# Layer boundary of a two-layer trunk: two tiles get the last expert block's rows from a product with a 0/1 matrix

## The chip, the cores and the metric

One core of one Trainium2 chip runs the whole kernel. The metric is the device time of one execution in microseconds. Before the change it is 2198.02 us, the median of three runs (2182.05 to 2208.55).

## What is computed

The reference is a decoder trunk of two layers on 1024 tokens of width 1024 in float32. Each layer is

```
h   = layer_norm(x) * (1 + sc1) + sh1
mix = concat(gating(h @ w_in), attention(h @ w_in), s5(h @ w_in)) @ w_out
x   = layer_norm(ALPHA * x + (1 + g1) * mix) * ln1_g + ln1_b
h2  = layer_norm(x) * (1 + sc2) + sh2
ffn = grouped_moe(h2)              # 16 experts, two for each token
x   = layer_norm(ALPHA * x + (1 + g2) * ffn) * ln2_g + ln2_b
```

The boundary between the layers is the last line of layer 0 with the first of layer 1: for each tile of 128 tokens one norm with `ln2_g`, `ln2_b`, and on its result another with layer 1's `sc1`, `sh1`. The product `h @ w_in` follows. The sum inside the last line is complete for a token only when both of its experts have added their rows.

## The kernel before

**Order of the work.** Every engine runs its instructions in the order in which the program emits them. That order comes from a planner (class `Flow`): tasks are generators with a priority (a lower number goes first), and the planner keeps its own clock of when each engine, transfer and buffer is free. A task that yields a time, an event or a buffer goes on when the planner's clock allows it. The planner's times decide the order alone; on the chip every instruction waits for its real inputs.

**End of layer 0.** Experts are taken in an order by their counts. Their tokens' rows of `h2` are gathered in blocks of 128 slots, go through gate, up (`expert`, L2033) and down (`down`, L2083), are weighted on VectorE, and are added to the running sum `xa` in DRAM by an indirect DMA of GpSimd (`add_rows`, L362). The last expert of the order, at place `HALVES`, has two blocks: the first holds tokens of the first half of the sequence (tiles 0 to 3), the second those of tiles 4 to 7. `settle` (L2591) notes the planner's time at which the adds of all other blocks are in (`settled[1]`), and then those of the first and of the second of these two blocks (`settled[0]`, `settled[2]`). It also sets `first_down`, when the first block's `down` task has ended; the splitting of layer 1's first weights is held until then (`hold`, L1033). Before layer 1 begins there is a loop with a run-time count for overfull experts (`over`, L2159), at which all engines meet.

**Entry of layer 1.** One task for each of the 8 tiles (`enter_on`, L1104, spawned at L2409 with priority 4.4): it waits for `settled[0]` (tiles 0 to 3) or `settled[2]` (tiles 4 to 7), loads 128 rows of `xa` (a slot of tag `hT`), takes mean and variance, applies `lg`, `lb` in two VectorE instructions, stores the result to `xres`, takes mean and variance again, and applies `sc`, `sh` in two VectorE instructions into a tile `t` of which there are two. Then eight PE transposes, each half copied and split into two parts by ScalarE and VectorE (`transpose_in`, L1054). Even tiles take their statistics on VectorE (`bn_stats`), odd ones on ScalarE (two passes with accumulation into a scratch half of the slot). The reciprocal root is seven small VectorE instructions (`rstd`, L393). With `steps` the task yields after each small instruction, so that several tiles' instructions interleave.

**The projection** (`project`, L1138, run by `first` at L2433) takes the tiles in order: for each, 24 products of 512 columns with the four units `uv` and 24 of 256 columns with the two units `us`. A unit is loaded into one of two buffers `raw` by SP's queue (`loader`) and split into two parts by ScalarE and VectorE (`splitter`, L1026).

**Buffers.** PSUM banks: three of kind A, two of B, two of Y, one of C. A block's `down` product takes both Y banks. The pool `hT` has 8 slots.

## Time and profile before

| | |
|---|---|
| Time, median of three runs | 2198.02 us (2182.05 to 2208.55) |
| The profiled execution's own time | 2191.28 us |
| Its span, first to last instruction | 2189.5 us |
| Mean granted TensorE clock | 0.942 of full speed |
| PE busy | 1931.7 us (88%) |
| DVE busy | 1191.8 us (54%) |
| ACT busy | 730.9 us (33%) |
| POOL busy | 317.8 us (15%) |

PE is TensorE's matmul side, PEld its weight loads, DVE VectorE, ACT ScalarE, POOL GpSimd, SP SyncE, whose queue issues most transfers. A busy share is an average over all stages. Almost every compute instruction goes through one of a few helpers, so its line is the helper's (L108 for DVE, ACT and POOL, L463 for products, L476 for transposes, L354 and L364 for transfers): one reads the groups by the names of their tiles. `bankA`, `bankB`, `bankC` and `bankY` are PSUM banks; `wu` and `hT` hold weights or activations; `xa` is the running sum in DRAM. The clock is given as a share of 2.4 GHz, so 0.50 is the lower level, 1.2 GHz. One fp32 product of 128x128 by 128x512 stands in the trace as two matmul records; a product of the split kind stands as one record.

### The profile page before, as it was taken

How to read it: one execution, taken by the hardware profiler on the slowest of the kernel's cores; microseconds unless marked ns; L12 is line 12 of the kernel's file. 1: busy time of each engine (PE TensorE's matmuls, PEld its weight loads, DVE VectorE, ACT ScalarE, POOL GpSimd, SP SyncE). 2: the span in 40 equal slices, each digit the busy share in tenths (PEclk: the TensorE clock that was granted, in tenths of full speed). 3: DMA queues.
4: the chain of work that ended last, by engine and by line, in shares of the span. 5: the costliest groups of instructions: out<-in, count | busy, mean ns of one | idle time of the engine just before them, and what ended most of it. 6: DMA issues, size and time to landing. Idle time of an engine off the chain costs nothing. (4 is left out here: it accounts for less than half of the span.)

```text
span 2189.5 us, 32472 instructions
## 1 busy us (share of the span) xinstructions
PE 1931.7 (88%) x12026; PEld 1343.3 (61%) x12026; DVE 1191.8 (54%) x2901; ACT 730.9 (33%) x1336; POOL 317.8 (15%) x304
## 2 busy tenths in 40 slices
PE   5988899999898999897867999999898999999882
PEld 3766676668663656556536877766685556665640
DVE  7757544556771754335368594445477432443636
ACT  2321144543321423324233424455223130332431
POOL 0014000100123323311001221020000111111010
PEclk9999999999999999999887999999899999999996
DMA  7566623245747799897763544331564678989782
GB/s 244 195 191 178 220 87 96 68 138 180 276 147 264 246 320 343 300 347 227 257 210 111 192 130 151 92 103 50 174 220 164 235 240 292 310 300 318 236 297 100
DMA packets 186822, 451.50 MB, mean 206 GB/s; under 512 B 28969, under 2 KB 80377, under 8 KB 169637
## 3 DMA queue, kind: packets, MB, share of 16 engines
q1 hardware_dynamic: 169584, 393.60, 51.3%
q0 software_dynamic: 15584, 55.24, 10.4%
q8 instruction: 96, 1.57, 0.3%
q10 hardware_dynamic: 1492, 0.56, 0.1%
q14 instruction: 66, 0.53, 0.1%
HBM read 366.66 MB, written 83.01 MB: 205 GB/s over the span
## 5 line engine op out<-in xcount | busy, mean ns | idle before, releaser
L463 PE MATMUL bankA<-wu,hT 128*128 128x512 f32 (+2 forms) x3250 | 832.3, 414 | 27.5 <-DMA hT<-mixT 12.8
L463 PEld LDWEIGHTS bankA<-wu,hT 128*128 128x128 f32 (+1 forms) x3250 | 565.9, 190 | 199.7 <-issue 67.7
L463 PE MATMUL bankA<-hT 128*128 128x512 f32 (+1 forms) x768 | 243.0, 482 | 3.0 <-DVE hT L108 1.9
L108 DVE TENSOR_TENSOR wu<-raw,wu 128x1024 fp32r<-128x1024 f32 x124 | 153.6, 1245 | 144.5 <-ACT wu L108 143.5
L108 ACT ACTIVATE hT<-bankB 128x512 fp32r<-128x512 f32 (+1 forms) x174 | 99.2, 594 | 354.5 <-PE bankB L476 335.0
L463 PE MATMUL bankY<-wu,hT 128*128 128x512 f32 (+1 forms) x500 | 187.7, 538 | 6.6 <-ACT hT L108 4.0
L108 ACT ACTIVATE wu<-raw 128x1024 fp32r<-128x1024 f32 x124 | 130.2, 1058 | 158.3 <-DMA raw<-in_exp_w_down_dram 33.4
L463 PEld LDWEIGHTS bankA<-hT 128*128 128x128 f32 (+1 forms) x768 | 131.5, 183 | 75.5 <-issue 48.6
L108 POOL TENSOR_TENSOR ada_w<-ada_w 128x512 f32<-128x512 f32 x84 | 118.4, 1409 | 351.9 <-ACT ada_w L108 342.8
L108 DVE TENSOR_TENSOR hT<-bankB,hT 128x512 fp32r<-128x512 f32 x114 | 75.8, 687 | 123.5 <-ACT hT L108 123.2
L463 PEld LDWEIGHTS bankY<-wu,hT 128*128 128x128 f32 (+1 forms) x500 | 93.4, 195 | 73.1 <-issue 52.0
L364 POOL DMA_INDIRECT xa<-g,rc_idx x40 | 70.7, 1767 | 459.5 <-DVE g L108 365.7
L463 PE MATMUL bankY<-hT 128*128 128x512 f32 (+1 forms) x404 | 117.5, 496 | 9.6 <-ACT hT L108 9.5
L108 DVE TENSOR_TENSOR hT<-raw,hT 128x1024 fp32r<-128x1024 f32 x57 | 70.4, 1238 | 87.9 <-ACT hT L108 87.3
L108 DVE SCALAR_TENSOR_TENSOR g<-bankY,rc_wsl,mod 128x512 f32<-128x512 f32 x68 | 48.4, 746 | 88.6 <-PE bankY L463 87.9
L463 PEld LDWEIGHTS bankY<-hT 128*128 128x128 f32 (+1 forms) x404 | 63.8, 179 | 48.4 <-issue 23.3
L108 ACT ACTIVATE ada_w<-ada_w,csel 128x512 f32<-128x512 f32 x96 | 67.5, 717 | 73.1 <-DMA ada_w<-in_ada_w_dram 71.4
L463 PE MATMUL bankC<-wu,hT 128*128 128x512 f32 (+1 forms) x260 | 83.4, 473 | 2.1 <-DVE wu L108 1.1
L108 ACT ACTIVATE hT<-raw 128x1024 fp32r<-128x1024 f32 x57 | 60.2, 1058 | 73.2 <-DMA raw<-in_exp_w_gate_dram 24.3
L108 ACT ACTIVATE hT<-hT,mx 128x256 f32<-128x256 f32 (+7 forms) x128 | 70.6, 557 | 6.3 <-DVE mx L108 6.2
L476 PE MATMUL bankB<-ident,hT 128*128 128x128 f32 x384 | 62.5, 289 | 7.1 <-ACT hT L108 3.9
L108 ACT ACTIVATE mhT<-bankB 128x512 f32<-128x512 f32 x32 | 19.1, 598 | 141.0 <-PE bankB L476 141.0
(495 smaller groups left out, 2608.7 us busy)
## 6 DMA issues: line engine op xcount, KB each, us to landing
ada_w<-in_ada_w_dram SPq DMA_DIRECT2D x160, 256.0 KB
raw<-in_exp_w_gate_dram SPq DMA_DIRECT2D x48, 512.0 KB
raw<-in_exp_w_up_dram SPq DMA_DIRECT2D x48, 512.0 KB
raw<-in_exp_w_down_dram SPq DMA_DIRECT2D x48, 512.0 KB
wu<-in_exp_w_up_dram SPq DMA_DIRECT2D x20, 1024.0 KB
wu<-in_exp_w_down_dram SPq DMA_DIRECT2D x19, 1024.0 KB
wu<-in_exp_w_gate_dram SPq DMA_DIRECT2D x19, 1024.0 KB
hT<-in_exp_w_up_dram SPq DMA_DIRECT2D x19, 1024.0 KB
```

Of the source, the lines that this page charges most:

```text
L108: f(*a, **k)
L364: self.nc.gpsimd.indirect_dma_start(out=rows, out_offset=bass.IndirectOffsetOnAxis(ap=ix, axis=0), in_=x, in_offset=None, compute_op=OP.add)
L463: self.nc.tensor.matmul(out, l, r, start=start, stop=stop, **kw)
L476: self.nc.tensor.transpose(out, x, self.ident[:k, :k] if perm is None else perm)
```

## The change

`enter_on` of tiles 0 and 1 (`HANDED` = 2) no longer waits for the first block of the last expert. It waits for `settled[1]`, reads its rows of `xa` without that block, and gets the block's share from PE: `place` builds for each of the two tiles a 128x128 matrix of zeros and ones (slot by token of the tile) in `rt["hx"]`; after the block's rows `y` are weighted, `down` multiplies each matrix with `y` into two Y banks, and `enter_on` adds the banks to its rows on VectorE and frees them. The scatter-add of that block is emitted only after both reads have been (`self.read`), and must not overwrite what they read. The two tasks get priority 0.5 in place of 4.4.

For all tiles: the slot of `x` is half as long; the tile `t` is taken before the first statistics instead of before the last affine step, and serves as ScalarE's scratch, so that every tile but tile 0 takes its statistics on ScalarE; tile i waits, ahead of its first affine step, until tile i-2's last affine step has been emitted (`entered`); tiles 0 and 1 run without `steps` and with fewer `pace` waits. In the planner every scatter-add of the kernel, in both layers, is taken to be done 6 us later.

```diff
--- before.py
+++ after.py
@@ -38,6 +38,8 @@
 EARLY = 2
 CAPS = (384,) + (256,) * 3 + (128,) * 2 + (64,) * 8 + (256,) + (128 * EARLY,)
 ALONE, HALVES, RANKED = 6, NE - 2, 5
+
+HANDED = 2
 BASE = [256 * EARLY + sum(CAPS[:p]) for p in range(NE - 1)] + [128 * EARLY]
 NPLAN = EARLY + sum(CAPS) // 128
 PAIRS = BASE[ALONE] // 128
@@ -363,7 +365,7 @@

         self.nc.gpsimd.indirect_dma_start(out=rows, out_offset=bass.IndirectOffsetOnAxis(ap=ix, axis=0), in_=x,
                                           in_offset=None, compute_op=OP.add)
-        return self.fl.dma("pool", rows, x, [ix])
+        return self.fl.dma("pool", rows, x, [ix]) + 6.0

     def to_row(self, dst, at, pool, tag):

@@ -443,6 +445,8 @@
             self.v.bn_aggr(mv[:, j], st.rearrange("p a b -> p (a b)"))
             if steps:
                 yield ("until", self.fl.busy["dve"])
+        if junk is not None and not steps:
+            yield self.fl.on(mv)
         rs = yield from self.rstd(tp, mv[:, :, 1], n, steps)
         return [(mv[:, j, 0:1], rs[:, j:j + 1]) for j in range(n)]

@@ -1103,29 +1107,45 @@

     def enter_on(self, l, i, tp, bc):

-        yield ("wait", self.settled[i * 2 // NT * 2])
-        x2 = yield ("tile", self.slots, [128, 2, D], F32, None)
-        x, junk = x2[:, 0], x2[:, 1] if i % 2 else None
+        yield ("wait", self.settled[1 if i < HANDED else i * 2 // NT * 2])
+        x = yield ("tile", self.slots, [128, D], F32, None)
         self.dma(x, self.xa[l - 1][i * 128:i * 128 + 128])
+        if i < HANDED:
+            self.unread -= 1
+            if not self.unread:
+                self.read.at = self.fl.now
+
+            pb, ev = self.handed[i]
+            yield ("wait", ev)
+            yield self.fl.on(x, *pb)
+            for n in range(2):
+                s = slice(n * 512, n * 512 + 512)
+                self.v.tensor_add(x[:, s], pb[n], x[:, s])
+            self.free(*pb)
         yield self.fl.on(x)
+        h = yield self.tile(tp, [128, D], F32, "t", 2)
         if i:
-            yield from self.pace(0.2)
-        st = yield from self.stats(tp, [x], D, junk, i > 0)
+            yield from self.pace(0.2, "act")
+        st = yield from self.stats(tp, [x], D, h if i else None, i >= 2)
         for k in ("lg", "lb"):
             yield ("wait", bc[k][1])
-        yield from self.pace(0.6)
+        if i > 1:
+            yield ("wait", self.entered[i - 2])
+        if i >= HANDED:
+            yield from self.pace(0.6)
         self.affine(x, x, st[0], bc["lg"][0], bc["lb"][0], x)
         yield self.fl.on(x)
         self.dma(self.xres[i * 128:i * 128 + 128], x)
         if i:
-            yield from self.pace(0.2)
-        st = yield from self.stats(tp, [x], D, junk, i > 0)
+            yield from self.pace(0.2, "act")
+        st = yield from self.stats(tp, [x], D, h if i else None, i >= 2)
         for k in ("sc", "sh"):
             yield ("wait", bc[k][1])
-        h = yield self.tile(tp, [128, D], F32, "t", 2)
-        yield from self.pace(0.6)
+        if i >= HANDED:
+            yield from self.pace(0.6)
         self.affine(h, x, st[0], bc["sc"][0], bc["sh"][0], h)
-        self.free(x2)
+        self.entered[i].at = self.fl.now
+        self.free(x)
         yield self.fl.on(h)
         yield from self.transpose_in(i, h)
         self.free(h)
@@ -1827,7 +1847,7 @@
         v.tensor_copy(r["ew"][:, a], tw[:, :, 1])
         self.ew_ready[j // 4].at = self.fl.on(r["ew"])[1]

-    def place(self, tp, xp):
+    def place(self, l, tp, xp):

         v, c, r = self.v, self.rc, self.rt
         mk = lambda s, sh, dt=F32: tp.tile(sh, dt, name="pl_" + s, tag="pl_" + s)
@@ -1912,6 +1932,13 @@
             self.free(oh, ob)
         at = mk("at", [128, NBLK])
         v.tensor_copy(at, pb[:, :NBLK])
+        if not l:
+
+            k, hx = BASE[HALVES] // 128, mk("hx", [128, HANDED])
+            r["hx"] = xp.tile([128, HANDED, 128], F32, name="hxs")
+            for i in range(HANDED):
+                v.tensor_scalar(hx[:, i:i + 1], at[:, k:k + 1], -1.0 - 128 * i, None, op0=OP.add)
+                v.tensor_scalar(r["hx"][:, i], c["i128"], hx[:, i:i + 1], None, op0=OP.is_equal)
         self.to_row(r["idx"], at, tp, "pl_t")
         self.idx_ready.at = self.fl.on(r["idx"])[1]
         v.tensor_scalar(at[:, PAIRS:NPLAN], at[:, PAIRS:NPLAN], c["hi"], None, op0=OP.mult)
@@ -2030,7 +2057,7 @@
                 self.mm(o[c], x[:, a, xk, c], u.part(b, uk), start and i == 0, stop and i == len(ps) - 1,
                         None if w == 128 else 0.43)

-    def expert(self, l, lanes, blocks, xes, ends, tp, early=False, keep=False, final=None):
+    def expert(self, l, lanes, blocks, xes, ends, tp, early=False, keep=False, final=None, hand=False):


         nu = len(lanes[0]) // 3
@@ -2074,13 +2101,13 @@
                                 self.free(gs[j])
                             if not early or xes[j].last:
                                 self.free(xes[j].tile)
-                            ends.append(self.fl.spawn(self.down(l, lanes, b, hid[j], pb[j], tp, work, final), 4))
+                            ends.append(self.fl.spawn(self.down(l, lanes, b, hid[j], pb[j], tp, work, final, hand), 4))
                     yield ("go",)
                 if not keep:
                     for u in us:
                         self.free(u.tile)

-    def down(self, l, lanes, b, hid, up, tp, work, final=None):
+    def down(self, l, lanes, b, hid, up, tp, work, final=None, hand=False):
         v, nu = self.v, len(lanes[0]) // 3
         yield self.fl.on(hid, up)
         v.tensor_mul(hid, hid, up)
@@ -2143,6 +2170,8 @@
         if early:
             for e in self.mix_done:
                 yield ("wait", e)
+        if hand:
+            yield ("wait", self.read)
         ix, xa = self.rt["eidx" if early else "idx"][:, b:b + 1], self.xa[l][:, :]
         if len(lanes) == 1:
             self.added.append(self.add_rows(xa, y, ix))
@@ -2150,6 +2179,13 @@

             self.add_rows(xa, y[0:64], ix[0:64])
             self.added.append(self.add_rows(xa, y, self.rt["idx2"][:, b - PAIRS:b - PAIRS + 1]))
+        if hand:
+            for i in range(HANDED):
+                pb, ev = self.handed[i]
+                pb += yield self.bank("Y", 2)
+                for n in range(2):
+                    self.mm(pb[n], self.rt["hx"][:, i], y[:, n * 512:n * 512 + 512], True, True)
+                ev.at = self.fl.now
         self.free(work)
         if b < EARLY:
             self.early_left -= 1
@@ -2392,7 +2428,7 @@
         self.hT_ready, self.s_ready, self.mix_done, self.chosen = ev(), ev(), ev(), ev(2)
         self.c_ready, self.b_left, self.left, self.late_left = Event(), [4] * NT, [4, 4], 2 * NT
         self.pa_open, self.kq_open, self.at_open, self.s5_go = ev(4)
-        self.vc, self.vc_ready = [None] * 2, ev(2)
+        self.vc, self.vc_ready, self.entered = [None] * 2, ev(2), ev()
         self.hT, self.q = [None] * NT, [None] * NT
         pa_s, kq_s = ExitStack(), ExitStack()
         b = SimpleNamespace(pa_s=pa_s, kq_s=kq_s, prep=None, sb=None)
@@ -2406,7 +2442,7 @@
             tp = self.pool(st, "prm", "right")
             loads = self.param_loads(tp)
         if l:
-            ins = [fl.spawn(self.enter_on(l, i, ln, bc), 4.4 + i / 100) for i in range(NT)]
+            ins = [fl.spawn(self.enter_on(l, i, ln, bc), (0.5 if i < HANDED else 4.4) + i / 100) for i in range(NT)]
         else:
             ins = [fl.spawn(self.enter(l, t, ln, bc), t[0]-2) for t in ((0,), (1,), (2, 3), (4, 5), (6, 7))]
         uv, us, ua = self.w_first
@@ -2568,7 +2604,7 @@
                 u.pools = self.wpools[:-1]
             self.g2 = self.mod(tp, l, 5, "g2")
             pl_s = ExitStack()
-            e = fl.spawn(self.place(self.pool(pl_s, "place", "right"), tp), 1)
+            e = fl.spawn(self.place(l, self.pool(pl_s, "place", "right"), tp), 1)
             fl.spawn(self.gather_first(l, 1, fx[EARLY:], [(tp, "g", 3)], tp), 0)
             runs = [early, fl.spawn(late_blocks(), 5.7)]
             for ps in ORDER:
@@ -2580,6 +2616,7 @@
             bh = [BASE[HALVES] // 128, BASE[HALVES] // 128 + 1]
             xh, written, first_up, first_down, emitted = ev(2), Event(), Event(), Event(), Event()
             settled = self.settled = ev(3)
+            self.read, self.unread, self.handed = Event(), HANDED, [([], Event()) for _ in range(HANDED)]
             for b, xe in zip(bh, xh):
                 fl.spawn(self.gather(l, b, xe, tp), 3)
             for u in ue[HALVES][4:]:
@@ -2606,7 +2643,7 @@
             def halves():
                 for k in range(2):
                     yield from self.expert(l, [ue[HALVES]], bh[k:k + 1], xh[k:k + 1], last, tp, keep=not k,
-                                           final=written if l else None)
+                                           final=written if l else None, hand=not l and not k)
                     if not k:
                         first_up.at = fl.now
             runs.append(fl.spawn(halves(), 5.5))
```

## Rows read from the trace of the kernel before

**Rows 1.** Waits, 1060 to 1250 us: who waited for whom; us, times, longest.
```profile
PE bankB L476 <- DVE t L108: 30.4, 2, 17.3
```

**Rows 2.** Timeline of PE, layer boundary: start, us, operation; idle before and releaser.
```profile
1106.43 7.03 PE L463 MATMUL bankA<-hT 128*128 128x512 f32 x16
...
1119.22 3.60 PE L463 MATMUL bankY<-wu,hT 128*128 128x512 f32 x8
...
1135.97 1.94 PE L476 MATMUL bankB<-ident,t 128*128 128x128 f32 x8 [13.15 <-DVE t L108]
...
1137.74 9.43 PE L463 MATMUL bankA<-wu,hT 128*128 128x512 f32 x48
...
1164.42 1.94 PE L476 MATMUL bankB<-ident,t 128*128 128x128 f32 x8 [17.26 <-DVE t L108]
...
1169.21 13.39 PE L463 MATMUL bankA<-wu,hT 128*128 128x512 f32 x60
...
1183.22 8.64 PE L463 MATMUL bankA<-wu,hT 128*128 128x512 f32 x48
...
1227.14 11.86 PE L463 MATMUL bankA<-wu,hT 128*128 128x512 f32 x61 [0.30 <-ACT hT L108]
```

**Rows 3.** Windows: length, busy us of PE, PEld, DVE, ACT, POOL; PE clock, DMA, GB/s.
```profile
1105.00:1240.00 135.00, 101.07 (x511) 80.03 (x510) 96.90 (x199) 54.38 (x104) 22.85 (x17) 0.86 0.48 154
...
1120.00:1180.00 60.00, 28.37 (x129) 22.98 (x128) 54.86 (x132) 19.86 (x42) 1.77 (x2) 0.69 0.51 178
...
1140.00:1150.00 10.00, 7.17 (x43) 6.20 (x41) 9.76 (x31) 6.81 (x16) 0.00 (x0) 0.99 0.46 181
...
1160.00:1170.00 10.00, 4.35 (x18) 3.88 (x19) 8.65 (x15) 2.20 (x4) 0.00 (x0) 0.50 0.14 56
```

**Rows 4.** Timeline of DVE, layer boundary.
```profile
1120.67 1.29 DVE L108 BATCH_NORM_STATS2 bn_s<-hT 128x6 f32<-128x512 f32 x2 [0.23 <-DMA hT<-xa]
...
1122.23 0.15 DVE L108 TENSOR_SCALAR rs_a<-bn_m 128x1 f32<-128x1 f32 x1
...
1126.21 1.40 DVE L108 SCALAR_TENSOR_TENSOR g<-bankY,rc_wsl,mod 128x512 f32<-128x512 f32 x2
...
1132.08 1.23 DVE L108 TENSOR_TENSOR wu<-raw,wu 128x1024 fp32r<-128x1024 f32 x1
...
1188.80 2.20 DVE L108 SCALAR_TENSOR_TENSOR t<-t,rs_y,mod 128x1024 f32<-128x1024 f32 x1
```

**Rows 5.** Timeline of POOL: a first gather, the last scatter-adds, a multiply-add of layer 1.
```profile
684.65 1.00 POOL L358 DMA_INDIRECT g<-h,rc_idx  x1 [0.15 <-issue]
...
1075.74 1.55 POOL L364 DMA_INDIRECT xa<-g,rc_idx  x1 [23.17 <-DVEq L2168]
...
1107.66 2.27 POOL L364 DMA_INDIRECT xa<-g,rc_idx  x1 [30.38 <-DVE g L108]
...
1190.28 1.87 POOL L108 TENSOR_TENSOR ada_w<-ada_w 128x512 f32<-128x512 f32 x1 [0.37 <-ACT ada_w L108]
```

**Rows 6.** Timeline of SP's DMA issues at the boundary.
```profile
1094.08 0.90 SPq L354 DMA_DIRECT2D mod<-modrow  x2
...
1108.55 1.52 SPq L354 DMA_DIRECT2D raw<-in_w_in_dram  x2
...
1117.45 1.76 SPq L354 DMA_DIRECT2D hT<-xa  x4
```

**Rows 7.** Groups of DVE, 1105 to 1240 us: operation, count, busy us, mean ns, idle before.
```profile
L108 DVE TENSOR_TENSOR wu<-raw,wu 128x1024 fp32r<-128x1024 f32 x9 | 11.2, 1259 | 11.3 <-ACT wu L108 11.3
```

**Rows 8.** Timeline of ACT: first and last instruction of an odd tile's statistics.
```profile
1129.28 1.04 ACT L108 ACTIVATE hT<-hT 128x1024 f32<-128x1024 f32 x1
...
1131.73 0.19 ACT L108 ACTIVATION_READ_ACCUMULATOR hT<-hT,bn_a 128x1 f32 x1
```

**Rows 9.** Timeline of DVE, layer 0's placing: the slot indices.
```profile
654.80 0.20 DVE L108 SCALAR_TENSOR_TENSOR rc_idx<-pl_at,pl_t 128x37 int32<-128x37 f32 x1
```

**Rows 10.** Timeline of DVE, last stage of layer 1.
```profile
2128.32 0.17 DVE L108 TENSOR_SCALAR rs_a<-bn_m 128x2 f32<-128x2 f32 x1 [9.01 <-ACT g L108]
```

## The prediction

> **What bounds the kernel now.** I read the page's shares first: PE is busy 88% of the span, DVE 54%. That says where the time goes on average, so the second view is the waits of the boundary, 1060 to 1250 us: PE stood 30.4 us in two pieces ahead of transposes that waited for DVE's tile `t` [rows 1]. The third is PE's timeline. The last block of layer 0 ends at 1122.8; tile 0's transposes start at 1135.97 after 13.15 us of idleness, its projection ends at 1147.17, then 17.26 us pass until tile 1's transposes at 1164.42; from 1169.21 PE is dense. Tile 7's projection is the first 48 of the 61 records from 1227.14, so it ends near 1227.14 + 48/61 x 11.86 = 1236.5 [rows 2]. The fourth is busy time by windows: from 1120 to 1180 DVE is busy 54.86 of 60 us, 91%, while PE is busy 28.37 [rows 3]. So the boundary is bound by DVE, which spends the first 60 us on norms of all tiles side by side while PE needs tile 1's. The reader should see two separate losses: tile 0 starts late, since its rows come back from DRAM only at 1120.67 [rows 4], 13 us after the block's scatter-add was issued at 1107.66 [rows 5]; and tile 1 is finished late, because tiles 2 to 7 share DVE with it.
>
> **The change, part by part.** I work out when tile 7's projection ends, against 1236.5.
>
> Start of DVE's work. The block's weighted rows are ready just before its add at 1107.66 [rows 5]. PE is then in the second block's up product, 16 records in 7.03 us from 1106.43 [rows 2]; the task gives PE away only after half of it, at 1109.9. Tile 0's product is two fp32 products, four records at 0.44 us: 1.8 us, so DVE can add at 1111.7. The two reads of `xa` need the last other add, issued at 1075.74 [rows 5], and stand on SP's queue behind the rows loaded at 1094.08; nothing follows there until 1108.55 [rows 6]. Before, four reads issued at 1117.45 [rows 6] let DVE start at 1120.67 [rows 4], 3.2 us later; even twice that puts the new ones in by 1102. They cost nothing; without that cover, the whole chain waits for them.
>
> DVE's work up to tile 7's transposed parts. In 1105 to 1240 DVE was busy 96.9 us [rows 3]. Tiles 2, 4 and 6 give six statistics to ACT: from 1120.67 to the first small instruction at 1122.23 is 1.56 us [rows 4], six are -9.4. Four adds out of PSUM come in; the nearest row is the weighting out of PSUM, two in 1.40 us at 1126.21 [rows 4], so +2.8. The first block's weighting lies ahead of the start: -1.4. Of nine splits of weights [rows 7] three lie behind the first projection, which needs six: at 1.23 us [rows 4], -3.7. The rest is 85.2 us.
>
> What share of the time DVE is busy. The bounds are 91% (the window with all tiles side by side) and 96.9/135 = 72% (the whole stage, where PE is the bound in its second half) [rows 3]. Two tiles `t` taken early mean two tiles in flight. From 1122.23 to 1126.21 a root and two affine steps take 3.98 us [rows 4], so a tile's DVE work is 2 x 3.98, with two part-subtractions from PSUM at 0.70 some 9.4 us. Its ACT statistics take 1129.28 to 1131.92, 2.64 us [rows 8], twice. A pair thus needs 18.8 us of DVE, and one tile's chain (9.4 + 5.3 + transposes 1.9 [rows 2]) is 16.6 us plus waits behind the other. I take 86%, nearer to 91%, because the work is the same: 85.2/0.86 = 99 us, to 1210.8. Tile 7 then needs its transposes, about 1.0 (half of the 1.94 at the lower clock), and 48 records at 8.64 [rows 2]: 1220. **Gain: 16 us.**
>
> Does PE allow that? Tile 0's chain took 1120.67 to 1135.97 [rows 2, 4]; from 1113.1 the same 15.3 us end at 1128.4. The weights' hold is released only after tile 1's product, about 1117 (another half product and 1.8 us) in place of 1107.7, so the sixth split, at 1132.08 before [rows 4], may be up to 10 us late; at worst tile 0's projection ends near 1144. Seven more tiles at 9.6 us end at 1211, before DVE's 1220. The hold therefore costs nothing unless DVE does better than 95%.
>
> Collisions with POOL. An affine step at 1188.80 took 2.20 us instead of 1.28 [rows 4]; POOL ran layer 1's multiply-adds, one from 1190.28 for 1.87 us [rows 5]. They are released by tile 3, which comes earlier, so more norms lie beside them; those met before are in the 96.9 already. I take 1 us, bounds 0 and 5 (0.92 us for about five more meetings). The Trainium skill ("SBUF — State Buffer", Who interferes with whom) says that a DVE instruction with two SBUF inputs and a POOL instruction that reads SBUF exclude each other for a whole instruction. The row agrees, and by that rule each meeting could cost up to 1.87 us, the sum losing 9 in place of 1.
>
> Costed at nothing. `place` gets four small DVE instructions, under 2 us, ahead of the slot indices; these are done at 655.0 [rows 9], and the first gather is issued at 684.65 [rows 5]. The products lengthen PE's queue by 3.5 us ahead of a 13.15 us gap. The second block's add, behind the first on POOL, is late by 4 to 7 us; it feeds tiles 4 to 7, needed after 1150. ACT takes 16 us more in a stage where it was busy 54.4 of 135 [rows 3]. The 6 us in the planner also reorder the last stage of layer 1, whose norms follow a scatter-add; no row shows that. There DVE waited 9.01 us behind ACT's statistics [rows 10]; later placing can add to that or fill it: -4 to +4, taken as 0.
>
> The sum is 15 us: 2191.3 - 15 = 2176.3 for the profiled execution. That lies 6.7 us under the median of 2198.0, so 2183 on the median's scale.
>
> **The rivals.** *DVE stays as dense as it was (chance 0.22).* At 91% the stage ends at 1111.7 + 93.6 + 9.6 = 1215; at best PE is the bound, with tile 0's projection over by 1140 and seven tiles at 9.6, 1207: a gain of 22 to 29 us, about 2173. For it: 91% was held for 60 us. Against: eight tiles in flight then, two now.
>
> *The reads come late, so the product gives no start (0.18).* The reads need free slots of `hT`. If there are none until the up weights' slots come free, when the 16 records end at 1113.5 [rows 2], the rows arrive near 1118, the block's add waits for them, and tiles 2 and 3 behind it: 6 us of start lost and a share near 80%, 85.2/0.8 = 106.5, end 1234: a gain of 2, so 2196.
>
> *Slower: two tiles in flight starve DVE (0.12).* DVE runs in order: an instruction waiting for ACT's statistics holds the other tile's ready ones, as for 9.01 us in the last stage [rows 10]. The break-even is 1236.5 = 1111.7 + 85.2/s + 9.6, a share s of 74%. PE would also idle ahead of each tile: the granted clock was 0.50 from 1160 to 1170, after the 17.26 us gap, against 0.99 from 1140 to 1150 [rows 3], and 60 records took 13.39 us, where 8.64 per 48 makes 10.8: 2.6 us for a restart [rows 2]. The last tile pays one. At 65%: 1111.7 + 131 + 9.6 + 2.6 = 1255, 18 us slower, 2216. The Trainium skill ("TensorE: Matmul & The Clock Gate", HAM oscillation) warns that matmuls fed in pieces with waits between fall back to the lower clock each time. The rows agree for single gaps; by it seven restarts at 2.6 us would cost PE 18 us, hidden as long as DVE is the bound.
>
> **How the numbers follow.** The forecast (share 80 to 91%, gain 8 to 22) has 0.48. Point: 2183. Range: from the dense rival at its best, 2169, with some of the runs' spread, 2163, to a share just past break-even, 2203. A measurement of this kernel can tell about 1%, 22 us. Faster by more, below 2176: most of the dense rival and the forecast's top with the runs' scatter, 0.32. Slower by more, past 2220, needs a share near 63%: 0.07. Within 1%: 0.61.
>
> **What would show it.** Right: DVE adds out of `bankY` near 1112; tile 0's transposes before 1131; tile 1's within 3 us of the end of tile 0's projection; DVE 80 to 91% busy from 1112 to 1205; dense PE from tile 1 on except gaps of 1 to 3 us that end on DVE `t`; tile 7's projection over near 1220. Wrong: reads of `xa` issued after 1105; a gap ahead of every tile with a clock below 1; DVE idle behind ACT; PE waiting for `wu`; a last stage of layer 1 longer or shorter by over 4 us.

## The result, and the profile after

The changed kernel takes **2174.67 us** (median of 4 runs, 2170.59 to 2178.52) beside 2202.56 us for the kernel before (4 runs): a ratio of 0.9897 [0.9861, 0.9933]. The forecast was 2183. The profiled execution took 2174.52 us (span 2172.7) against 2191.28, so 17 us went. Where they went is not where the forecast had them. I measure the **stage** from the end of the first block's weighting on DVE to ACT's reading of tile 7's last bank: 128.7 us before, 120.7 after. That is 8 us; the forecast had 16, less 1 for collisions. Another 14 us are gone before the boundary begins, and 5.5 us come back behind it.

POOL's timeline of the changed kernel shows the last other add and the two adds of the last expert:

```profile
1061.40 1.55 POOL L366 DMA_INDIRECT xa<-g,rc_idx  x1 [24.05 <-DVEq L2204]
1093.51 1.55 POOL L366 DMA_INDIRECT xa<-g,rc_idx  x1 [30.56 <-DVE g L110]
1122.31 1.55 POOL L366 DMA_INDIRECT xa<-g,rc_idx  x1 [27.25 <-DVE g L110]
```

Against [rows 5] the last other add is issued 14.3 us earlier and the block's 14.2 us earlier. Nothing of the boundary has happened when the first of them is issued. SP's timeline answers to [rows 6]:

```profile
1080.45 1.06 SPq L356 DMA_DIRECT2D hT<-xa  x2
...
1104.07 1.25 SPq L356 DMA_DIRECT2D hT<-xa  x2
```

The rows of tiles 0 and 1 are read ahead of the block's add. PE's timeline at the boundary answers to [rows 2]:

```profile
1095.54 1.88 PE L467 MATMUL bankY<-g,hxs 128*128 128x512 f32 x4
...
1100.69 1.88 PE L467 MATMUL bankY<-g,hxs 128*128 128x512 f32 x4
...
1106.60 1.13 PE L480 MATMUL bankB<-ident,hid 128*128 128x128 f32 x4 [4.03 <-DVE hid L110]
...
1116.03 1.04 PE L480 MATMUL bankB<-ident,t 128*128 128x128 f32 x8
...
1128.75 1.94 PE L480 MATMUL bankB<-ident,t 128*128 128x128 f32 x8 [2.49 <-DVE t L110]
...
1131.99 11.44 PE L467 MATMUL bankA<-wu,hT 128*128 128x256 f32 x59 [0.68 <-DVE wu L110]
1145.06 1.07 PE L480 MATMUL bankB<-ident,t 128*128 128x128 f32 x8 [1.62 <-DVE rs_a L110]
...
1191.24 1.94 PE L480 MATMUL bankB<-ident,t 128*128 128x128 f32 x8 [3.60 <-DVE rs_a L110]
1193.02 6.13 PE L467 MATMUL bankA<-wu,hT 128*128 128x512 f32 x18
...
1200.89 14.24 PE L467 MATMUL bankA<-wu,hT 128*128 128x512 f32 x84
```

The two gaps of [rows 2], 13.15 and 17.26 us, are gone. Gaps of 1.6 to 3.6 us ahead of single tiles stand in their place; `rs_a` as releaser is the small instruction that follows the tile's affine step on DVE. Tile 7's projection ends with the 78th of the last 84 records, near 1214.1, counted as in the forecast. The waits of the same stretch (1060 to 1250 us) answer to [rows 1]:

```profile
PE bankB L480 <- DVE rs_a L110: 8.0, 5, 3.6
PE bankB L480 <- DVE hid L110: 4.0, 1, 4.0
PE bankB L480 <- DVE t L110: 3.4, 2, 2.5
```

The 4.0 us on `hid` are new at this place, where the kernel before waited 0.78 us (at 1114.25): the second block's hidden product stands on DVE behind tile 0's norm. The windows answer to [rows 3]; the first one runs from DVE's first add out of `bankY` to the end of tile 7's parts:

```profile
1096.60:1202.70 106.10, 87.86 (x421) 66.87 (x420) 88.30 (x180) 63.14 (x132) 18.99 (x15) 0.90 0.53 168
...
1120.00:1180.00 60.00, 51.66 (x283) 43.31 (x282) 49.07 (x107) 43.50 (x94) 11.72 (x9) 0.94 0.58 183
```

From 1120 to 1180 PE is now busy 51.66 us in place of 28.37, and DVE 49.07 in place of 54.86. But the boundary begins 14.3 us earlier now, so these 60 us don't hold the same part of the work. The window of the kernel before that lies 14.3 us later is the fair one, and against it PE is busy 12 us more and DVE about as long as before:

```profile
1134.30:1194.30 60.00, 39.85 (x204) 34.46 (x205) 50.18 (x124) 23.49 (x50) 3.37 (x3) 0.76 0.39 142
```

DVE's timeline answers to [rows 4]:

```profile
1096.60 0.69 DVE L110 TENSOR_TENSOR hT<-bankY,hT 128x512 f32<-128x512 f32 x1 [3.54 <-PE bankY L467]
...
1105.87 0.68 DVE L110 TENSOR_TENSOR hid<-hid,bankA 128x512 f32<-128x512 f32 x1
...
1152.68 1.29 DVE L110 TENSOR_TENSOR hT<-bankB,hT 128x512 fp32r<-128x512 f32 x2 [1.38 <-ACT hT L110]
...
1188.93 2.17 DVE L110 SCALAR_TENSOR_TENSOR t<-t,rs_y,mod 128x1024 f32<-128x1024 f32 x1
...
1194.76 1.10 DVE L110 SCALAR_TENSOR_TENSOR rs_y<-rs_t,rs_g 128x1 f32<-128x1 f32 x1
```

In the last stage of layer 1 the wait behind ACT [rows 10] is unchanged:

```profile
2111.64 0.17 DVE L110 TENSOR_SCALAR rs_a<-bn_m 128x2 f32<-128x2 f32 x1 [9.02 <-ACT g L110]
```

### The profile page after: what moved, and what is told of

The parts are those of the page before. It is cut to its first block, busy times and chain, and to the rows that moved or that the text cites. A ratio compares the mean times of both kernels' runs of the same rounds, so it can differ in the third digit from the quotient of the medians.

```text
span 2172.7 us, 32497 instructions
## 1 busy us (share of the span) xinstructions
PE 1939.7 (89%) x12034; PEld 1341.7 (62%) x12034; DVE 1186.0 (55%) x2891; ACT 747.2 (34%) x1372; POOL 312.0 (14%) x304
## 5 line engine op out<-in xcount | busy, mean ns | idle before, releaser
L467 PE MATMUL bankA<-hT 128*128 128x512 f32 (+1 forms) x834 | 260.2, 476 | 10.3 <-ACT hT L110 6.7
L467 PE MATMUL bankY<-wu,hT 128*128 128x512 f32 (+1 forms) x584 | 207.1, 520 | 5.0 <-ACT hT L110 4.1
L467 PEld LDWEIGHTS bankA<-hT 128*128 128x128 f32 (+1 forms) x834 | 143.4, 183 | 81.8 <-issue 43.5
L110 ACT ACTIVATE wu<-raw 128x1024 fp32r<-128x1024 f32 x122 | 128.8, 1060 | 157.3 <-DMA raw<-in_exp_w_gate_dram 40.6
L467 PEld LDWEIGHTS bankY<-wu,hT 128*128 128x128 f32 (+1 forms) x584 | 104.0, 188 | 76.3 <-issue 54.9
L110 DVE TENSOR_TENSOR hT<-raw,hT 128x1024 fp32r<-128x1024 f32 x61 | 75.9, 1249 | 86.0 <-ACT hT L110 85.6
L467 PE MATMUL bankY<-hT 128*128 128x512 f32 (+1 forms) x310 | 104.1, 511 | 8.7 <-ACT hT L110 8.4
L467 PEld LDWEIGHTS bankY<-hT 128*128 128x128 f32 (+1 forms) x310 | 53.8, 189 | 46.1 <-issue 24.0
```

Of the source, the lines that this page charges most:

```text
L110: f(*a, **k)
L467: self.nc.tensor.matmul(out, l, r, start=start, stop=stop, **kw)
```

## The experiments

Each was timed in five rounds beside the kernel before on the same chip (chips differ between groups). The stage is that of each kernel's one profile. The ratio does not go by the medians alone: a's stands for 19.3 us, its medians for 23.4, and m's for 17.8 beside 14.1. So a gain of a few us below is known to some 4 us.

| Kernel | what it has | us, median | before | ratio | stage, us |
|---|---|---|---|---|---|
| a_same | the whole change | 2172.62 | 2196.03 | 0.9912 [0.9882, 0.9942] | 121.6 |
| b_no_handing | all but the product | 2196.67 | 2196.03 | 1.0001 [0.9979, 1.0023] | 128.0 |
| c_handing_only | product, tiles 2 to 7 old | 2176.49 | 2196.03 | 0.9928 [0.9903, 0.9953] | 128.2 |
| d_no_6us | all but the 6 us | 2178.93 | 2196.03 | 0.9926 [0.9899, 0.9953] | 126.5 |
| e_hx_only | before, matrices built | 2191.58 | 2196.81 | 0.9972 [0.9953, 0.9991] | 128.3 |
| j_yield_only | before, `stats` waits | 2189.71 | 2196.81 | 0.9972 [0.9957, 0.9988] | 128.3 |
| k_hx_late | change, matrices built late | 2182.54 | 2196.81 | 0.9938 [0.9914, 0.9961] | 121.1 |
| l_no_yield | change, no wait in layer 0 | 2184.21 | 2196.81 | 0.9934 [0.9910, 0.9959] | 122.7 |
| m_order_only | before, e and j together | 2181.40 | 2195.51 | 0.9919 [0.9897, 0.9940] | 129.1 |
| h_three_deep | change, three in flight | 2176.46 | 2195.51 | 0.9901 [0.9874, 0.9929] | 124.5 |
| g_hold_early | change, hold released early | 2180.03 | 2195.51 | 0.9914 [0.9888, 0.9940] | 120.0 |
| n_boundary_only | change without e and j | 2187.41 | 2196.50 | 0.9953 [0.9934, 0.9971] | 120.9 |

**a_same.** The changed kernel once more, no edit.

> The changed kernel again, beside the kernel before on the same chip. Its first trace has three differences: the first block's scatter-add is issued 14.2 us earlier (1093.5 against 1107.7), the boundary stage from that add to the end of tile 7's projection is 8.2 us shorter (120.6 against 128.8), and 5.6 us are lost after it. Boundary theory (mine): the stage of 8 us is the change's, the 14 us ahead of it are scatter between executions, so here 5 to 12 us in all, ratio 0.9945 to 0.998. Rival, layer 0: the 14 us come from another order of layer 0's expert stage and are there every time: 15 us or more, ratio 0.9935 or less.

The gain holds, and the block's add again comes early, at 1095.77 in its profile: the 14 us ahead of the boundary are not scatter, as I had thought, and the rival's case, 15 us or more, is what came.

**b_no_handing.** The two tiles read their rows back; single slots, ACT's statistics, two tiles in flight and the 6 us stay.

```diff
-HANDED = 2
+HANDED = 0
-        if not l:
+        if not l and HANDED:
...
-    hand=not l and not k)
+    hand=HANDED > 0 and not l and not k)
```

> The changed kernel without the product: no tile is handed rows, tiles 0 and 1 wait for the first block's add like tiles 2 and 3; the two-tile depth, ACT statistics and the 6 us stay. Boundary theory: the start is given up, so the first VectorE statistics come 13 us behind the add instead of 3; with tile 1 still finished early about half of the stage's gain stays: stage 125 to 132 us, 4 to 10 us slower than the changed kernel. Rival, that the depth of two is the whole gain: the stage stays within 2 us of 120.6.

Nothing is left of the gain: 24 us against a, where 4 to 10 were expected. The edit takes away more than the product, though: without `HANDED` no matrices are built in `place` either. I first read this run as proof for the boundary, which it isn't.

**c_handing_only.** Tiles 2 to 7 enter as before the change.

```diff
+        if i >= HANDED:
+            yield from self.enter_old(l, i, tp, bc)
+            return
```

> The changed kernel with tiles 2 to 7 entering as before (all side by side, statistics alternating between VectorE and ScalarE, tile t taken late, no wait for the tile two ahead); tiles 0 and 1 get the product. Boundary theory: tiles 0 and 1 start early and go first by their priority, but tiles 2 to 7 then share VectorE, so a gap of 8 to 15 us opens ahead of tile 2; VectorE's share rises to 88% or more and the stage ends within 4 us of the changed kernel's 120.6. Rival, that the wait for the tile two ahead carries the gain: stage 126 us or more.

Most of the time gained, but a stage as long as before, so on the stage the rival (126 us or more) is right. Its PE timeline, with the second tile's start and the gaps that follow:

```profile
1124.66 1.06 PE L480 MATMUL bankB<-ident,t 128*128 128x128 f32 x8 [2.48 <-DVE t L110]
...
1146.70 1.94 PE L480 MATMUL bankB<-ident,t 128*128 128x128 f32 x8 [6.37 <-DVE t L110]
...
1165.32 1.94 PE L480 MATMUL bankB<-ident,t 128*128 128x128 f32 x8 [5.01 <-DVE t L110]
```

Tile 1 is early, and then DVE works on six tiles side by side and PE waits for the next ones. In b's timeline it is the other way round: one long gap for tile 0, and none for tile 1.

```profile
1131.94 1.94 PE L480 MATMUL bankB<-ident,t 128*128 128x128 f32 x8 [18.32 <-DVE t L110]
...
1142.14 1.04 PE L480 MATMUL bankB<-ident,t 128*128 128x128 f32 x8
```

In these profiles neither half shortens the stage (128.2 and 128.0); the two together do. And a gain of nearly 20 us with a stage of the old length means that something else pays.

**d_no_6us.** The planner takes a scatter-add to be done as early as before.

```diff
-        return self.fl.dma("pool", rows, x, [ix]) + 6.0
+        return self.fl.dma("pool", rows, x, [ix])
```

> The changed kernel without the 6 us that the planner adds to every scatter-add. Boundary theory: the 6 us decide only the order at the boundary and in the last stage of layer 1; without them tiles 2 and 3 are planned too early and their instructions stand ahead of ready ones on VectorE and SP: stage 2 to 6 us longer; the last stage (from the last block's down product of layer 1 to the end) moves by less than 4 us either way. Rival, layer 0: everything ahead of the boundary moves back by 10 us or more.

The time can't be told from a's; the stage of its profile is 126.5 us, 5 us longer than a's as expected, with a gap of 5.58 us ahead of tile 1 on PE. SP's timeline and DVE's show how:

```profile
1085.88 19.64 SPq L356 DMA_DIRECT2D hT<-xa  x4
```
```profile
1133.87 1.28 DVE L110 SCALAR_TENSOR_TENSOR hT<-hT,bn_m,lg 128x1024 f32<-128x1024 f32 x1
...
1137.84 1.28 DVE L110 SCALAR_TENSOR_TENSOR t<-hT,bn_m,mod 128x1024 f32<-128x1024 f32 x1
```

With the earlier time the planner puts the reads of tiles 2 and 3 right behind those of 0 and 1, and a later tile's first affine step ahead of tile 1's last one. In the changed kernel tile 1's last step comes first.

**What b had mixed up.** The lists of instructions told the next theory. The change moves the order of the work in *layer 0*, twice. `stats` now gives up its turn once the statistics are in, and layer 0's first norms, for the pairs of tiles, call it too: in the traces of j and of the kernel before, PE's order differs from about 78 us on. And the four DVE instructions for the matrices in `place` shift the planner's clock: between e and the kernel before, PE's order differs from about 685 us on, up to the boundary. The next five kernels tell the theories "the boundary pays" and "the new order ahead pays" apart.

**e_hx_only.**

```diff
+        if not l:
+            k, hx = BASE[HALVES] // 128, mk("hx", [128, 2])
+            r["hx"] = xp.tile([128, 2, 128], F32, name="hxs")
+            ...
```

> The kernel before, with the 0/1 matrices built in `place` as in the change and used by nothing. The program's order of the work on PE, DVE and SP is then another one from `place` to the boundary, since the planner sees four more DVE instructions; at the boundary itself tiles 0 and 1 are read back as before. Theory 'the boundary pays' (the product and what it starts early give the gain): the time of the kernel before, 2196 +- 3 us, ratio 1.00. Theory 'the new order ahead of the boundary pays' (the gain comes with the matrices and would be there without the product): 2175 +- 4 us, ratio 0.990. Between them, near 2186, each would have half.

Neither: 5.2 us by the medians. **j_yield_only**, in `stats`:

```diff
+        if junk is not None and n > 1:
+            yield self.fl.on(mv)
         rs = yield from self.rstd(tp, mv[:, :, 1], n, steps)
```

> The kernel before with only that wait in `stats` for the pairs of tiles that enter layer 0, nothing at the boundary and no matrices. Both main theories: 2196 +- 4 us, ratio 1.00. Third theory, 'the wait in layer 0 carries part of it': 2186 to 2191, ratio 0.996.

The third theory: 7.1 us. **k_hx_late** builds the matrices at the first block's hidden product:

```diff
+        if hand:
+            hx, r = self.hx1, self.rt
+            for i in range(HANDED):
+                v.tensor_scalar(hx[:, i:i + 1], r["idx"][:, b:b + 1], -128.0 * i, None, op0=OP.add)
+                v.tensor_scalar(r["hx"][:, i], self.rc["i128"], hx[:, i:i + 1], None, op0=OP.is_equal)
```

> The changed kernel, with the four DVE instructions that build the 0/1 matrices moved out of `place` to the hidden product of the first block of the halves, some 430 us later. Up to the boundary the order of the work on every engine is then that of the kernel without handing (b_no_handing, 2196.67 us); at the boundary the product is used as in the change. Theory 'the boundary pays': the changed kernel's time, 2174 +- 4 us, ratio 0.990, and the stretch from the block's add to the end of tile 7's projection near 120 us in the profile. Theory 'the new order ahead pays': 2195 +- 4 us, ratio 1.00.

In the middle between both. **l_no_yield:**

```diff
-        if junk is not None and not steps:
+        if junk is not None and not steps and n == 1:
             yield self.fl.on(mv)
```

> The changed kernel without the wait that its `stats` gained for the pairs of tiles that enter layer 0; the wait moves the order of PE's work in layer 0 from its 20th row on. Both theories on the boundary and on the matrices: no difference, 2174 +- 4 us, ratio 0.990, since the kernel without handing had this wait and the time of before. Third theory, 'the wait in layer 0 carries part of it': some 5 to 10 us more than the changed kernel, 2179 to 2184.

Again the third theory. With and without the product, at the same order ahead, the medians differ by 7.4 us (l and e) and 7.2 us (k and j): that is what the boundary gives, and about what the stages show (5.6 and 7.2 us). **m_order_only**, both edits of e and j and nothing at the boundary:

> The kernel before with both things that move the order of layer 0 (the wait in `stats` for the pairs, and the 0/1 matrices built in `place`, used by nothing), and nothing of the change at the boundary: tiles 0 and 1 are read back, statistics and slots are the old ones. Theory 'two gains': the new order ahead gives 12 us (5 + 6 of the two single runs) and the product 8, so 2184 +- 4 us, ratio 0.9945, the block's add near 1096 us and the stage from it to tile 7's end still near 128 us. Theory 'the boundary alone, the single runs were luck': 2194 +- 3 us. Theory 'the order alone': 2175 +- 4 us.

14.1 us without any change at the boundary, whose stage stays at 129.1. **n_boundary_only**, the edits of k and l together, is its complement:

> The boundary of the change alone: the product, the single slots, the statistics on ACT and two tiles in flight, but no wait in `stats` for layer 0's pairs and the 0/1 matrices built only at the first block's hidden product, so that up to the boundary the order of the work is that of the kernel before. The forecast's own sum: the stage 16 us shorter, 2181 +- 3 us. Theory 'two gains': the stage near 120 us in the profile instead of 128, 2 us given back in layer 1, 2189 +- 4 us, ratio 0.9965. Theory 'the order alone': 2196 +- 3 us.

9.1 us, as "two gains" has it; the ratio's interval allows 6.4 to 14.5 us and ends short of the forecast's 15.5. By the medians the two add up to 23.2 us, and the whole change was worth 23.4 in a. By the ratios it is 17.8 and 10.3 beside 19.3 us, each known to 4 to 7 us: the two sums agree, but no closer than that.

Where the order ahead pays can be seen. PE's waits of n from 195 to 350 us, where the order is still that of the kernel before, hold these lines:

```profile
PE bankB L480 <- DVE q L110: 4.7, 1, 4.7
...
PE bankB L480 <- DVE gt L110: 3.9, 1, 3.9
PE bankA L467 <- ACT q L110: 3.5, 1, 3.5
```

The changed kernel's largest entry there is 1.9 us, in two waits. PE's busy time from 100 to 350 us, of n and then of m:

```profile
100.00:350.00 250.00, 225.94 (x1527) 171.86 (x1526) 148.78 (x491) 63.42 (x111) 38.97 (x66) 0.95 0.52 168
```
```profile
100.00:350.00 250.00, 232.12 (x1547) 174.89 (x1547) 148.21 (x486) 66.03 (x116) 36.45 (x66) 0.97 0.52 167
```

The four profiles with the old order have 225.9 to 226.8 us, the ten with the new one 231.6 to 233.2. What that is worth can be read off an instruction that every kernel has, the slot indices [rows 9]. In DVE's timelines of n and of m it stands at:

```profile
654.13 0.20 DVE L110 SCALAR_TENSOR_TENSOR rc_idx<-pl_at,pl_t 128x37 int32<-128x37 f32 x1
```
```profile
644.14 0.20 DVE L108 SCALAR_TENSOR_TENSOR rc_idx<-pl_at,pl_t 128x37 int32<-128x37 f32 x1
```

With the old order it starts at 653.0 to 654.8 us (four profiles), with the new one at 644.1 to 651.0 (ten): 7.4 us earlier by the means. The matrices act later: PE's wait for the first gathered blocks (670 to 705 us), in the profiles of k (built late) and of a:

```profile
PE bankB L480 <- DMA g<-h,rc_idx: 4.7, 1, 4.7
```
```profile
PE bankB L480 <- DMA g<-h,rc_idx: 0.9, 1, 0.9
```

Without them it is 4.0 to 4.7 us in five profiles, with them 0 to 2.9 in nine. From the slot indices to the end of the first block's weighting those five take 452.6 to 461.0 us and those nine 443.0 to 452.9, 7.4 us less by the means. So both parts of the 14 us are seen where the order differs; single profiles scatter by as much as the parts, and which of the moved instructions carries the gain is shown at these places alone.

**h_three_deep.** The scratch goes back into the slot, `t` is taken late, and a tile waits for the one three ahead.

```diff
-            yield ("wait", self.entered[i - 2])
+            yield ("wait", self.entered[i - 3])
...
-            st = yield from self.stats(tp, [x], D, h if i else None, i >= 2)
+            st = yield from self.stats(tp, [x], D, junk if i else None, i >= 2)
```

> The changed kernel with three tiles in flight in the boundary instead of two: the statistics' scratch goes into the tile's slot, so that the tile `t` is taken late, and a tile waits for the one three ahead. Theory 'DVE stands behind ACT because only two tiles are in flight': DVE's share of 83% in the stage rises to 90%, its 106 us fall to 98, 2167 +- 4 us. Rival 'DVE runs its queue in order, and more tiles only lengthen the queue in front of the ready instruction': the stage stays at 118 to 124 us, 2174 +- 4 us, or is longer by up to 5.

The rival: no faster (2176.46), the stage 124.5 us, 3 to 4 us longer than the changed kernel's. DVE's stretch and PE's largest wait in the stage:

```profile
1100.37:1208.88 108.51, 87.62 (x414) 67.10 (x413) 88.35 (x180) 62.55 (x131) 16.32 (x14) 0.87 0.50 162
```
```profile
PE bankB L480 <- DVE t L110: 11.3, 3, 6.9
```

DVE's share is 81%, no higher. The wait for the tile two ahead was not run by itself, so its own part is not shown; two tiles `t`, taken early, hold the third back as well.

**g_hold_early.** The first weights of layer 1 are released at the block's add.

```diff
+            self.first_down.at = self.fl.now
             for i in range(HANDED):
```

> The changed kernel with layer 1's first weights released as the block's add is issued and not behind the two products. If the hold costs nothing, as was forecast: 2174 +- 4 us, ratio 0.990. If the late weights hold PE in the stage: the waits of PE for wu (0.2 and 0.7 us) go and 1 to 3 us are gained, 2172.

2180.03, above both expectations (2174 +- 4 and 2172), with an interval that holds a's ratio, and a stage of 120.0 us. The hold costs nothing that can be measured.

## Why the total was right and its parts were not

*The reads come in time: right, but closely.* In n, where nothing ahead has moved, they are issued at 1097.25, before the bound of 1105. Their way was sized wrong: the forecast took twice 3.2 us at most, in by 1102, but by the landing events of n's trace they are in at 1108.5 and 1109.8, 11.3 and 11.8 us after their issue. Tile 0's rows have 3 us to spare before DVE's add at 1111.49, and not 10. And the block's add must wait for that landing. POOL's timeline of n:

```profile
1110.57 1.54 POOL L366 DMA_INDIRECT xa<-g,rc_idx  x1 [31.06 <-DMA hT<-xa]
```

The weighting had ended at 1107.95, so 2.6 us. The product doesn't wait for the add (it started at 1110.43), so tile 0 is not late; of the rival "the reads come late" that much is true.

*Start of DVE's work: right.* 3.1 us after the block's scatter-add in the changed kernel; 4.0 were forecast. The product's four records take 1.88 us (1.8).

*The DVE work: 88.3 us where 86.2 were forecast (85.2 and 1 for collisions).* The collisions with POOL did not grow. From 1096.60 to 1202.70 one affine step took 2.17 us instead of 1.28, and five small instructions of `rstd` took 0.57, 0.58, 1.01, 1.02 and 1.10 us instead of 0.16, each beside a multiply-add on POOL: 4.4 us together. Five more affine steps met such an instruction and kept their 1.28 us; each had begun before it. But the stage of the kernel before (1105 to 1240) has 5.9 us of the same kind, three affine steps and four small instructions, and these are in the 96.9: 1.5 us less, not 1 more. The Trainium skill ("SBUF — State Buffer", Who interferes with whom) names DVE instructions with two SBUF inputs, and all six are of that kind; the small `TENSOR_SCALAR` between them, with one, keep their 0.27 us. The 1.87 us for each meeting that the forecast worked out by that rule were not reached: the longest of the six cost 0.94 us.

The other terms came as costed: by the durations of the groups the statistics give -9.4 us, the adds +2.8, the weighting -1.5, the splits -4.0. What failed is what the sum took for granted, that the rest of the work stays as it is. With all tiles side by side the small instructions of one tile's root ran while another's still did. In DVE's timeline of the kernel before the second of these starts 0.09 us ahead of the end of the pair in the first, and the third before the second has ended:

```profile
1144.29 0.21 DVE L108 TENSOR_SCALAR rs_a<-bn_m 128x1 f32<-128x1 f32 x2
1144.41 0.16 DVE L108 SCALAR_TENSOR_TENSOR rs_y<-rs_t,rs_g 128x1 f32<-128x1 f32 x1
1144.49 0.21 DVE L108 TENSOR_SCALAR rs_g<-rs_a 128x1 int32<-128x1 int32 x2
```

In the changed kernel one tile's chain runs alone, each instruction behind the one before:

```profile
1153.88 0.15 DVE L110 TENSOR_SCALAR rs_g<-rs_a 128x1 int32<-128x1 int32 x1
1154.07 0.27 DVE L110 TENSOR_SCALAR rs_t<-rs_a,rs_g 128x1 f32<-128x1 f32 x1
```

The kernel before has 45 such overlaps between small instructions, 3.6 us in its stage, and the changed kernel has none, while c, whose tiles 2 to 7 run side by side, has 44 from 1092 to 1205; over all of DVE's instructions the overlap falls from 9.3 to 4.9 us. That is more than the 2.1 us that were missing.

*The share of DVE's time: 83%, where 86% was forecast.* Both lie in the band that was given (80 to 91%), but 106.1 us instead of 100 (99 and the 1 us of collisions) is most of what is missing. Of the 17.8 us in which DVE is idle, nearly half is one wait, of the changed kernel from 1096 to 1203 us (16.1 us in the kernel before, from 1105 to 1240):

```profile
DVE hT L110 <- ACT hT L110: 8.4, 7, 1.6
```

DVE's subtraction waits for ACT's copy out of PSUM, and the other tile's ready instructions stand behind it. That was on the list of what would make the forecast wrong. What the share would be without this wait no run shows.

*Tile 7 behind DVE: 11.4 us instead of 9.6.* Its 48 records stand behind 30 of tile 6. So the stage: 1.0 us better at the start, 6.0 worse in DVE's stretch (2.4 by the work, 3.6 by the share), 1.8 worse at the end, 6.8 together; 15 becomes 8. The rest of the step was as described: tile 0's transposes 22.5 us after the add (under 23.3), tile 1's 2.5 us behind tile 0's work, dense PE with short gaps.

*The rivals at the boundary fell.* DVE did not stay as dense as it was (83%, not 91), and it did not starve (74% was the break-even).

*Costed at nothing, and here the forecast failed.* "`place` gets four small DVE instructions, under 2 us": their own time is nothing, but they and the wait in `stats` move the planner's order, and m shows 14.1 us from that alone. The forecast looked for cost and never for a gain, and it took the wait in `stats` for part of the boundary, though layer 0 runs the same function. The 6 us that reorder the last stage: its wait is 9.02 us as before. From ACT's reading of tile 7's last bank to the end the changed kernel takes 958.9 us, the kernel before 953.4; the other profiles have 956.0 to 959.6 without the product and 957.1 to 961.8 with it (h: 953.5), their medians differ by 1 us, less than either group scatters, so it is not shown that any of the 5.5 us belong to the change. So the forecast came near by luck. For the profiled execution it was 2176.3, and 2174.5 were measured: 7 us too many at the boundary, and 14 us ahead of it and 5.5 behind it that had no term, nearly cancelled. By the medians the gain was 23.4 us in a, where 15 were forecast.

*Open:* b has the order ahead of j and of k, gains nothing, and its stage is no longer than j's. Its interval and j's overlap in [0.9979, 0.9988], but k's does not reach it: with the product k is some 14 us better than b, twice what their stages differ by (121.1 and 128.0). b's one profile can't tell, since it is of its fastest run (2184.51 beside a median of 2196.67); in it the slot indices come at 644.97, as early as in m. So the 7 to 9 us of the boundary rest on l, k and n, and b does not fit them.

## What to carry to other kernels

Where a planner writes the order, a change has as many places as its order has differences: compare the two lists of instructions before costing, and put a term of either sign for every stage in which they differ. An experiment that takes a part out must leave the order elsewhere alone, or it measures both; run the complement too, and see whether the two add up. More tiles in flight don't by themselves make a limiting engine denser: here DVE was busy 83% of the stretch with two and 81% with three. And work that overlapped while many tiles ran side by side costs more when they run one behind the other: a sum of busy times carries that overlap with it.

## What the runs showed of the hardware

The reads of `xa` are issued 18.8 to 20.5 us after the last other scatter-add was (9 profiles with the product). That is not the add's price alone: its landing came 10.0 to 11.4 us after its issue (12 profiles that show it). SP stands in the loop at which all engines meet (L2204), and then issues `lg`, `lb` and `mod`; the reads follow these without a wait of their own. The changed kernel's longest waits of SP from 1050 to 1100, and SP's timeline around them:

```profile
SPq L2204 <- SPq L2204: 17.8, 2, 16.5
```
```profile
1053.29 2.46 SPq L356 DMA_DIRECT2D raw<-in_w_in_dram  x2
1078.65 0.34 SPq L356 DMA_DIRECT2D lg<-in_ln_g_dram  x1
```

By the landing events of that trace the four loads come in one after another, from 1082.3 to 1090.4, and the two reads behind them at 1091.5 and 1092.7. That is 10.8 to 11.8 us after their issue in all nine profiles, where the first two reads of the kernel before, with nothing issued for 7 us ahead of them, took 3.2 and 4.1 us.

Not every short gap sent PE's clock down. Of the changed kernel's five gaps above 1 us in the stage, those of 1.62 and 2.06 us left it at its upper level, and the transposes behind them took 1.07 and 1.06 us; behind those of 2.49, 3.60 and 4.03 us the granted clock was 0.50, 1.2 GHz, and the eight transposes behind the first two took 1.94. The length of the gap does not decide alone: gaps of 2.48 us in c and of 2.50 us in n left the clock at 1.00. Windows behind the gaps of 1.62 and of 3.60 us, the clock third from the end:

```profile
1145.00:1150.00 5.00, 4.69 (x23) 3.56 (x24) 3.62 (x10) 3.61 (x8) 0.00 (x0) 1.00 0.55 180
...
1191.20:1196.00 4.80, 4.75 (x15) 3.93 (x16) 2.92 (x6) 2.53 (x4) 2.38 (x3) 0.50 0.34 102
```

The last one's price is also in the 18 records that took 6.13 us, where 18 behind the gap of 1.62 us took 4.65. The Trainium skill ("TensorE: Matmul & The Clock Gate", HAM oscillation) tells of a kernel whose clock falls back at every wait between its pieces of matmul work; here three of five did it.
